# First norms on ScalarE, both parts of the forget weights side by side, and the cumulative sums placed later, in a two-block transformer kernel

## The chip, the cores and the metric

The kernel runs on one core of one Trainium2 chip. The metric is the device time of one execution in microseconds, taken as the median of several runs.

## The reference

Two transformer blocks work on 256 tokens of width 1024; in the first, 16 learned meta tokens stand ahead of them, so L = 272. Only the head of the first block matters here:

```python
h = jnp.concatenate([meta, x], axis=1)
hn = rms_norm(h, ln_pre_mix[layer])
proj = jnp.einsum('bld,dc->blc', hn, w_in[layer])
...
f_b = proj[..., OFF_VB:] + b_forget[layer].astype(proj.dtype)
o_a = swa_sink_attention(q_a, k_a, v_a, sinks[layer], rel_bias)
o_b = forgetting_attention(q_b, k_b, v_b, f_b)
```

`forgetting_attention` has 8 heads. It forms `cum = cumsum(log_sigmoid(f_logit))` along the sequence and adds `cum[t] - cum[s]` to the score of query t and key s. `swa_sink_attention` has 8 query heads and 2 key heads, a window of 128 tokens, and a bias per head that is read from a table of 32 buckets by distance. Behind both stand the output projection, a feed-forward part, and the second block.

## The kernel before, in words

All activations of the first block are kept transposed, as 8 slices of 128 channels by 272 tokens. Each number is held as a high part (`xh`, rounded to the format that TensorE takes at full speed) and a low part (`xl`, the rest). Weights are split in the same way when they have been loaded: `load` (L107) issues a transfer on SP's queue into one of three buffers `x`, ScalarE writes the high part `hi` (L114), and VectorE or GpSimd subtracts it for the low part `lo` (L115). A projection of one weight tile is then 8 x 3 products: high by high, high by low, low by high (L151 to L153).

`start` (L289) loads the meta rows and the tokens, forms the sum of squares of each row, and from it the factor of the norm. The factor goes onto the diagonal of a 128 x 128 matrix, and a product of the token rows with it scales and transposes at once (L327). Then the gain of the norm is applied (L621), the high part taken by ScalarE (L622) and the low part by VectorE or GpSimd (L623). Within the `with self.in_order(...)` block the order on VectorE, ScalarE and TensorE is the order of the code.

`first_block` (L684) follows. It projects the forget logits (weights `w_f`, 8 columns), then the tiles of `w_in` in the order of the plan at L692: tiles 6 to 9 are the queries of the forgetting attention, 10 to 13 its keys, 14 to 17 its values, 0 to 5 belong to the window attention. `uq(c)` projects tile 6 + c, `uk(c)` tile 10 + c. `cumulate1` transposes the log-sigmoids `fz` and `cumulate2` sums them by products with a triangular matrix; ScalarE copies the sums into `cum` and the negated ones into `ncum`, and two transfers on GpSimd's queue put them into row 64 of `qf` (queries) and row 65 of `kf` (keys). The scores of one pair of heads (L452) are products of 66 rows of `qf` and `kf`, so they add the sums by themselves, and they need both transfers.

`t5_bias` builds the bias of the window attention: a product with the bucket table, a copy by ScalarE into `t5qa` (L421), a transfer into DRAM (`t5vec`, L423), one that makes 32 copies of it there (`t5scr`, L426), and 16 that read these with shifted offsets into `bias` (L433). All of these are issued on GpSimd's queue (POOL), one behind the other.

The attention of four head pairs and then of four more runs as a pipeline of steps; `fills` names what is projected in each step. A step's fills stand ahead of the scores of its pair. Outside of the block that keeps the order of the code, a scheduler decides in which order each engine's instructions, and those of the queues, are written; on the chip each engine and each queue then takes them in that order.

Of the kernel before, what the change touches and what calls it, by code (L numbers as in the profile page):

```python
# [10 lines left out]
F32 = mybir.dt.float32  # L11
F32R = mybir.dt.float32r
# [4 lines left out]
AF = mybir.ActivationFunctionType  # L17
OP = mybir.AluOpType
AX = mybir.AxisListType
DRAM = bass.MemoryType.DRAM  # L20

D = 1024
# [24 lines left out]
NE1 = 'DDDD'  # L47
NE2='DADA'
NE3 = 'DDDD'
WM0 = 13  # L50
WM2 = 0
XO = 0
T5C = 32
# [11 lines left out]
FA = 1  # L65
FB = 0
FO = 0
CA, CB = 2, 3
KLT = 4
LATF = (12, 14, 16, 18)  # L70

C_PRE_MIX, C_PRE_FFN, C_BADA, C_C, C_QN, C_KVN, C_OA, C_OB = 0, 8, 16, 64, 72, 74, 75, 79
NCOLS = 83


class Body:
# [129 lines left out]
    def setup(self):  # L206
        nc, t, c = self.nc, self.t, self.const
        self.eps = c.tile([128, 1], F32, name="eps")
        nc.vector.memset(self.eps, EPS)

        nc.scalar.activation(self.sm([128, 1]), self.eps, AF.Sqrt)
        self.ident = c.tile([128, 128], F32, name="ident")
        self.cols = c.tile([128, NCOLS], F32, name="cols")

        self.xhb = c.tile([128, KT * L1 + NM], F32R, name="xh")
        self.xlb = c.tile([128, KT * L1 + NM], F32R, name="xl")
        self.xh, self.xl = (x[:, :KT * L1].rearrange("p (k n) -> p k n", k=KT) for x in (self.xhb, self.xlb))
        self.csil = c.tile([128, KT], F32, name="csil")
        self.modT = c.tile([128, 32], F32, name="modT")
        self.nx, self.nh, self.nl = 3, 4, 4  # L220
        self.rooms = False
        self.strm = self.ctx.enter_context(self.tc.tile_pool(name="strm", bufs=1, reuse_waits="tile"))

        self.hctx = ExitStack()
        hp = self.hctx.enter_context(self.tc.tile_pool(name="hp", bufs=1, reuse_waits="tile"))
        self.h = hp.tile([128, 2, D], F32, name="h")
        self.rn = hp.tile([128, T], F32, name="rn")
        self.ones = hp.tile([128, 128], F32, name="ones")
        nc.gpsimd.memset(self.ones, 1.0)
        self.hd = self.dram.tile([128, 2, D], F32, name="hd")  # L230
# [58 lines left out]
    def start(self, pool):  # L289

        nc, t = self.nc, self.t

        m = pool.tile([128, 4, T], F32, name="meta", tag="qa")[:NM].rearrange("p a b -> p (a b)")
        nc.sync.dma_start(m, t["meta"])
        half = [slice(hf * 512, (hf + 1) * 512) for hf in range(2)]
        for tt in range(2):
            for d in half:
                nc.sync.dma_start(self.h[:, tt, d], t["x"][tt * 128:(tt + 1) * 128, d])
        nc.sync.dma_start(self.ident, t["ident"])
        nc.sync.dma_start(self.cols, t["cols"])  # L300
        sm = self.sm([128, 1])[:NM]
        ym = pool.tile([128, KT, NM], F32, name="ymeta")
        y = pool.tile([128, 8, 288], F32, name="y", tag="bias").rearrange("p a b -> p (a b)")
        y = y[:, :2 * D].rearrange("p (t k n) -> p t k n", t=2, k=KT)
        gain = self.cols[:, C_PRE_MIX:C_PRE_MIX + KT, None]

        def norm(tt):

            ss, v, q, s = (self.sm([128, 1], tag=f"start{n}", bufs=2) for n in range(4))
            a, b = (self.h[:, tt, d] for d in half)  # L310
            self.square_sum(ss, a)
            nc.vector.tensor_scalar(v, ss, 1.0 / D, EPS, op0=OP.mult, op1=OP.add)
            sc = pool.tile([128, 2, 512], F32, name=self.nm("sqv"), tag="vf")[:, 0]
            nc.vector.tensor_tensor_reduce(sc, b, b, 1.0, 0.0, op0=OP.mult, op1=OP.add, accum_out=q)
            nc.scalar.activation(s, q, AF.Sqrt, scale=1.0 / D, bias=v)
            nc.vector.scalar_tensor_tensor(v, q, 1.0 / D, v, op0=OP.mult, op1=OP.add)
            return s, [lambda: nc.vector.reciprocal(s, s), lambda: nc.vector.tensor_mul(q, s, s),
                       lambda: nc.vector.scalar_tensor_tensor(q, q, -0.5, v, op0=OP.mult, op1=OP.mult),
                       lambda: nc.vector.scalar_tensor_tensor(s, q, 1.5, s, op0=OP.add, op1=OP.mult)]

        def scaled(x, n, r, banks, w):

            d = pool.tile([128, 128], F32, name=self.nm("diag"), tag="diag", bufs=3)[:n, :n]
            nc.vector.tensor_scalar(d, self.ident[:n, :n], r, None, op0=OP.mult)
            for k in range(KT):
                p, o = banks[k // w], k % w * n
                nc.tensor.matmul(p[:, o:o + n], lhsT=x[:, k * 128:(k + 1) * 128], rhs=d, start=True, stop=True)  # L327

        def gained(p, tt, hf, low, later=None):
            k, o = slice(hf * 4, hf * 4 + 4), tt * (128 + NM)  # L330
            self.gained(p[hf], y[:, tt, k], C_PRE_MIX + hf * 4, self.xh[:, k, o:o + 128], self.xl[:, k, o:o + 128], low, later)

        pw = self.bank()
        pm = self.bank()
        p0, p1 = ([self.bank() for _ in range(2)] for _ in range(2))
        mt = slice(128, 128 + NM)
        with self.in_order(mybir.EngineType.PE):
            self.warm(WM0, pw)
            self.square_sum(sm, m)
            rm = self.rstd(sm, 1, D)  # L340
            r0, steps = norm(0)
            for f in steps:
                f()
            scaled(self.h[:, 0], 128, r0, p0, 4)
            scaled(m, NM, rm, [pm], KT)
            r1, steps = norm(1)
            steps.pop(0)()
            gained(p0, 0, 0, nc.gpsimd)
            for f in steps:
                f()  # L350
            scaled(self.h[:, 1], 128, r1, p1, 4)
            gained(p0, 0, 1, nc.gpsimd)
            nc.vector.tensor_tensor(ym, pm[:, :KT * NM].rearrange("p (k n) -> p k n", k=KT),
                                    gain.to_broadcast([128, KT, NM]), op=OP.mult)
            nc.scalar.activation(self.xh[:, :, mt], ym, AF.Copy)
            nc.vector.tensor_sub(self.xl[:, :, mt], ym, self.xh[:, :, mt].bitcast(F32))
            self.fetch(1, nc.vector)
            if FO == 0:
                self.fetch(1, nc.gpsimd)
            self.warm(WM2, pw)  # L360
            late = []
            gained(p1, 1, 0, nc.vector, late)
            if FO == 1:
                self.fetch(1, nc.gpsimd)
            gained(p1, 1, 1, nc.vector, late)
            if FO == 2:
                self.fetch(1, nc.gpsimd)
            for f in late:
                f()
            self.fetch(1, nc.vector)  # L370

    def proj(self, out, wh, wl, apart):

# [252 lines left out]
    def scaled(self, xn, r, tt, hf):  # L626

        d = slice(hf * 512, (hf + 1) * 512)
        self.nc.vector.tensor_scalar(xn[:, d], self.h[:, tt, d], r, None, op0=OP.mult)
        return self.transposed4(xn, hf)  # L630
# [53 lines left out]
    def first_block(self):  # L684
        nc, t = self.nc, self.t
        w = self.work
        def win(*cs):
            return [("w_in", c, 1024) for c in cs]

        def wout(*cs):  # L690
            return [("w_out", c, 1024) for c in cs]
        self.plan(("w_f", None, 64), *win(6, 10, 7, 11, 8, 12, 9, 13, 14, 15, 4, 16, 5, 0, 17, 1, 2, 3),  # L692
                  *wout(4, 5, 6, 7, 0, 1, 2, 3))
        actx = ExitStack()
        self.attn = A = actx.enter_context(self.tc.tile_pool(name="attn1", bufs=1, reuse_waits="tile"))
# [4 lines left out]
        nc.gpsimd.memset(kf[64:66], 1.0)  # L700
        zz = A.tile([128, 5, 32], F32, name="zz")
        nc.gpsimd.memset(zz, 0.0)
        self.start(A)
        self.bias = A.tile([128, 8, 288], F32, name="bias", tag="bias")
        nc.sync.dma_start(bf, t["b_forget"])

        f = self.proj_tile("w_f", m=8, n=L1)
        z = A.tile([8, L1], F32, name="fz")
        nc.scalar.activation(z, f, AF.Identity, bias=bf)
        az = A.tile([8, L1], F32, name="faz")  # L710
# [66 lines left out]
                late.pop(0)()  # L777

        def uq(c):
            p = self.proj_tile("w_in", 6 + c, real=True)  # L780
            flush()
            for hd in range(2):
                nc.scalar.activation(qf[:64, 2 * c + hd], p[hd * 64:(hd + 1) * 64], AF.Copy, scale=0.125)

        def uk(c):
            p = self.proj_tile("w_in", 10 + c, n=L1)
            flush()
            for hd in range(2):
                nc.scalar.activation(kf[:64, 2 * c + hd], p[hd * 64:(hd + 1) * 64], AF.Copy)
# [48 lines left out]
        for i, (f, c) in enumerate(((uq, 0), (uk, 0), (uq, 1), (uk, 1))):  # L838
# [5 lines left out]
        vf = A.tile([128, 2, 512], F32, name="vf", tag="vf")  # L844
        do = lambda f, *a: (lambda: f(*a))
        fills = {
            0: [do(uq, 2), do(uk, 2)],
            1: [do(uq, 3), do(uk, 3), do(uv, 0)],
            2: [do(uv, 1), uka],
            3: [do(uv, 2), uva, do(uqa, 0)],  # L850
            4: [do(uv, 3), do(uqa, 1)],
# [25 lines left out]
        def gained(p, tt, hf, by, later=None):  # L877
            k, q = slice(hf * 4, hf * 4 + 4), slice(tt * 128, (tt + 1) * 128)
            self.gained(p[hf], y[:, tt, hf], C_PRE_FFN + hf * 4, self.xh[:, k, q], self.xl[:, k, q], by, later)
# [993 lines left out]
```

## Time and profile before

| | |
|---|---|
| median of 3 runs | 1260.43 us (1260.41 to 1262.22) |
| the profiled execution, its time | 1261.71 us |
| its span, first to last instruction | 1259.4 us |
| TensorE busy (PE) | 1230.8 us, 98% |
| VectorE busy (DVE) | 959.1 us, 76% |
| ScalarE busy (ACT) | 679.9 us, 54% |
| GpSimd busy (POOL) | 30.9 us, 2% |
| mean granted clock of TensorE | 0.997 |

Times in the profile count from the span's start. A busy TensorE may hide short waits, since the ends of products are modelled. In a row of the timeline the start stands first, then the duration of the group, the engine, the line, the operation, what it writes and reads, and how many instructions the group has; in square brackets the idle time ahead of it and what ended it. "SPq" and "POOL ... DMA" are issues of transfers.

### The profile page before, as it was taken

The numbers are of one execution on the slowest core, as the hardware profiler recorded it, in microseconds if no ns is written. First come the engines' busy times: TensorE is split into PE (matmuls) and PEld (weight loads), VectorE is DVE, ScalarE is ACT, GpSimd is POOL, SyncE is SP. The second block draws the span as 40 slices with busy tenths as digits, with TensorE's granted clock in tenths as the row PEclk, the third lists the DMA queues.
The fourth block names the chain that finished last, engine by engine and source line by source line (L and its number), as shares of the span: only waits on it lengthen the run. The fifth ranks groups of instructions, "written<-read, shape, count | busy, mean of one in ns | idle before, by whom it ended". The sixth has DMA issues, their size and how long they took to land.

```text
span 1259.4 us, 22080 instructions
## 1 busy us (share of the span) xinstructions
PE 1230.8 (98%) x8424; PEld 1102.8 (88%) x8424; DVE 959.1 (76%) x1923; ACT 679.9 (54%) x1268; POOL 30.9 (2%) x40
## 2 busy tenths in 40 slices
PE   8999999999999999999999999999999999999997
PEld 7887899999785499999999999999988888888885
DVE  5679887787878669998889999997555855555555
ACT  6655644454667355447566655545445545445453
POOL 2300200000000000000000000000000000000000
PEclk9999999999999999999999999999999999999999
DMA  6756588878261156565555544556676866656662
GB/s 223 212 203 220 178 289 281 272 264 296 83 191 62 34 191 198 176 188 174 171 165 166 152 153 151 158 151 196 197 253 212 306 199 189 197 184 189 196 195 90
DMA packets 67845, 239.44 MB, mean 190 GB/s; under 512 B 8499, under 2 KB 9155, under 8 KB 67452
## 3 DMA queue, kind: packets, MB, share of 16 engines
q1 hardware_dynamic: 66236, 233.00, 57.7%
q0 software_dynamic: 1216, 4.51, 1.2%
q8 instruction: 66, 1.08, 0.3%
q10 hardware_dynamic: 288, 0.52, 0.1%
q14 instruction: 39, 0.32, 0.1%
HBM read 235.87 MB, written 2.79 MB: 190 GB/s over the span
## 4 chain that ended last, share of the span: by engine, by line
PE 72%; DVE 15%; ACT 5%; DMA 5%; issue 3%; SPq 0%; POOL 0%; ACTq 0%; DVEq 0%
PE ps L151 19%; PE ps L153 19%; PE ps L152 19%; DVE lo L115 4%; ACT hi L114 3%; DVE W L1596 3%; PE ps L574 2%; DMA x<-in_w_gu 2%; PE ps L377 2%; PE ps L379 2%; PE ps L380 2%; PE ps L452 1%; DMA x<-in_w_down 1%; DVE al L1579 1%; PE ps L507 1%
## 5 line engine op out<-in xcount | busy, mean ns | idle before, releaser
L115 DVE TENSOR_TENSOR lo<-x,hi 128x1024 fp32r<-128x1024 f32 (+2 forms) x373 | 451.1, 1212 | 195.8 <-ACT hi L114 193.0
L114 ACT ACTIVATE hi<-x 128x1024 fp32r<-128x1024 f32 (+2 forms) x376 | 394.1, 1051 | 347.2 <-PE ps L153 171.0
L151 PE MATMUL ps<-xh,hi 128*128 128x256 f32 (+2 forms) x1296 | 373.6, 288 | 1.0 <-ACT xh L622 1.0
L152 PE MATMUL ps<-xl,hi 128*128 128x256 f32 (+2 forms) x1296 | 364.1, 281 | 1.5 <-DVE xl L623 1.5
L153 PE MATMUL ps<-xh,lo 128*128 128x256 f32 (+2 forms) x1296 | 364.4, 281 | 0.0
L152 PEld LDWEIGHTS ps<-xl,hi 128*128 128x128 f32 (+1 forms) x1296 | 244.0, 188 | 2.0 <-POOL lo L115 1.7
L151 PEld LDWEIGHTS ps<-xh,hi 128*128 128x128 f32 (+1 forms) x1296 | 243.2, 188 | 2.0 <-ACT xh L622 1.2
L153 PEld LDWEIGHTS ps<-xh,lo 128*128 128x128 f32 (+1 forms) x1296 | 243.3, 188 | 0.4 <-DVE lo L115 0.2
L151 PE MATMUL ps<-hi,w 128*128 128x512 f32 x512 | 199.6, 390 | 0.0
L153 PE MATMUL ps<-hi,w 128*128 128x512 f32 x512 | 199.2, 389 | 0.0
L152 PE MATMUL ps<-lo,w 128*128 128x512 f32 x512 | 199.2, 389 | 0.0
L152 PEld LDWEIGHTS ps<-lo,w 128*128 128x128 f32 x512 | 96.1, 188 | 20.2 <-issue 0.2
L151 PEld LDWEIGHTS ps<-hi,w 128*128 128x128 f32 x512 | 96.1, 188 | 20.1 <-ACT hi L114 0.2
L153 PEld LDWEIGHTS ps<-hi,w 128*128 128x128 f32 x512 | 96.1, 188 | 19.9
L377 PE MATMUL ps<-xh,hi 128*128 128x256 f32 x352 | 99.4, 283 | 0.6 <-ACT xh L622 0.6
L380 PE MATMUL ps<-xh,lo 128*128 128x256 f32 x352 | 98.6, 281 | 0.0
L379 PE MATMUL ps<-xl,hi 128*128 128x256 f32 x344 | 96.7, 281 | 0.0
L1598 ACT ACTIVATE W<-ps 128x352 f32<-128x352 f32 (+31 forms) x64 | 35.2, 554 | 68.8 <-DVE W L1596 68.7
L377 PEld LDWEIGHTS ps<-xh,hi 128*128 128x128 f32 x352 | 66.2, 188 | 1.6 <-ACT xh L622 0.9
L380 PEld LDWEIGHTS ps<-xh,lo 128*128 128x128 f32 x352 | 66.3, 188 | 0.0
L379 PEld LDWEIGHTS ps<-xl,hi 128*128 128x128 f32 x344 | 64.9, 189 | 0.7
L1596 DVE SCALAR_TENSOR_TENSOR W<-ps,W 128x160 f32<-128x160 f32 (+31 forms) x64 | 54.7, 861 | 11.8 <-ACT W L1635 11.5
(365 smaller groups left out, 1578.2 us busy)
## 6 DMA issues: line engine op xcount, KB each, us to landing
x<-in_u SPq DMA_DIRECT2D x128, 512.0 KB, 3.6
x<-in_v SPq DMA_DIRECT2D x128, 512.0 KB, 4.2
x<-in_w_gu SPq DMA_DIRECT2D x44, 512.0 KB, 4.5
ada<-in_w_ada SPq DMA_DIRECT2D x40, 512.0 KB, 5.0
x<-in_w_down SPq DMA_DIRECT2D x22, 512.0 KB, 4.4
x<-in_w_in SPq DMA_DIRECT2D x18, 512.0 KB, 4.3
x<-in_w_out SPq DMA_DIRECT2D x16, 512.0 KB, 4.4
x<-in_w_query SPq DMA_DIRECT2D x16, 512.0 KB, 3.6
```

Of the source, the lines that this page charges most:

```text
L114: nc.scalar.activation(hi[:, :w], x[:, :w], AF.Copy)
L115: low.tensor_sub(lo[:, :w], x[:, :w], hi[:, :w].bitcast(F32))
L151: mm(out, lhsT=lh, rhs=rh, start=start, stop=False)
L152: mm(out, lhsT=lh, rhs=rl, start=False, stop=False)
L153: mm(out, lhsT=ll, rhs=rh, start=False, stop=stop)
L377: mm(out, lhsT=wh[:, s], rhs=self.xh[:, k, :T], start=k == 0, stop=False)
L379: mm(out, lhsT=wh[:, s], rhs=self.xl[:, k, :T], start=False, stop=False)
L380: mm(out, lhsT=wl[:, s], rhs=self.xh[:, k, :T], start=False, stop=not apart and k == KT - 1)
L452: nc.tensor.matmul(S[tl, hd], lhsT=qT(tl, hd), rhs=kT(hd, n), start=True, stop=True)
L574: self.nc.tensor.matmul(acc[tt][hf], lhsT=o[:, tt * 128:(tt + 1) * 128], rhs=w[:, hf * 512:(hf + 1) * 512], start=start, stop=stop)
L1596: nc.vector.scalar_tensor_tensor(a, pv[:, :, :i0], 1.0 / GSC, a, op0=OP.mult, op1=OP.mult)
L1598: nc.scalar.activation(W[:, i0:, tk].rearrange("p i t -> p t i"), pv[:, :, i0:], AF.Copy, scale=1.0 / GSC)
```

## The change

- The meta rows are loaded on ScalarE's queue, the token rows come first on SP's, the identity matrix between the two row tiles. The forget weights get a buffer of their own (`wfx`), not one of the three for weight tiles.
- Squares of the tokens are summed by ScalarE alone, those of the meta rows by VectorE. The meta rows are scaled by ScalarE with their factor and then transposed, behind both token tiles, where before they went through a diagonal matrix between them. Warming products: 11 ahead and 4 behind, where 13 stood ahead.
- All low parts of this norm, and of the first weight tiles, are VectorE's; GpSimd computes nothing there.
- High and low part of the forget weights stand side by side as 16 columns. They are multiplied with `xh` and `xl` (16 products where 24 stood), and a product with `sel` adds the two halves.
- The projections of tiles 6 and 10 are written out in the ordered block, part by part: all products with high parts first.
- `cumulate1` runs behind `uk(1)` where it ran ahead of it; `cumulate2` is a fill of the first step behind `uq(2)`, where it ran ahead of `t5_bias`. `uq(3)` is moved from the second step into the first, so ahead of the first scores.

```diff
-WM0 = 13
+WM0 = 11
...
-CA, CB = 2, 3
+CA, CB = 3, 4
...
-        nc.sync.dma_start(m, t["meta"])
+        nc.scalar.dma_start(m, t["meta"])
+
+        nc.scalar.activation(self.sm([128, 1]), self.eps, AF.Sqrt)
...
-        nc.sync.dma_start(self.ident, t["ident"])
+            if tt == 0:
+                nc.sync.dma_start(self.ident, t["ident"])
         nc.sync.dma_start(self.cols, t["cols"])
+        self.wf = pool.tile([128, KT, 8], F32, name="wfx")
+        nc.sync.dma_start(self.wf, t["w_f"].rearrange("p (k n) -> p k n", k=KT))
...
+        def products(p, n, w, x, start=False, stop=False):
+
+            o = p[:, :n]
+            if n == T:
+                o = o.rearrange("p (a b) -> p a b", a=2)
+            for k in range(KT):
+                b = x[:, k * L1:k * L1 + n] if n == L1 else x[:, k * L1:k * L1 + 288].rearrange("p (a b) -> p a b", a=2)[:, :, :128]
+                mm(o, lhsT=w[:, k * 128:(k + 1) * 128], rhs=b, start=start and k == 0, stop=stop and k == KT - 1)
+
+        wf = pool.tile([128, KT, 2, 8], F32R, name="wf")
+
+        def forget(x, start=False, stop=False):
+
+            for k in range(KT):
+                mm(pf[:16, :L1], lhsT=wf[:, k].rearrange("p s n -> p (s n)"), rhs=x[:, k], start=start and k == 0, stop=stop and k == KT - 1)
...
+            scaled(self.h[:, 1], r, p1)
+            nc.scalar.activation(m, m, AF.Copy, scale=rm)
+            for k in range(KT):
+                nc.tensor.transpose(pm[:, k * NM:(k + 1) * NM], m[:, k * 128:(k + 1) * 128], self.ident[:NM, :NM])
+            nc.scalar.activation(wf[:, :, 0], self.wf, AF.Copy)
+            nc.vector.tensor_sub(wf[:, :, 1], self.wf, wf[:, :, 0].bitcast(F32))
+            self.warm(4, pw)
+            late = []
+            for tt, p in enumerate((p0, p1)):
+                for hf in range(2):
+                    gained(p, tt, hf, nc.vector, late)
...
+            self.fetch(3, nc.vector)
+            uq, uk = self.unit("w_in", 6, False), self.unit("w_in", 10, False)
+            forget(self.xh, start=True)
+            products(pq, T, uq[0], self.xhb, start=True)
+            forget(self.xl, stop=True)
+            nc.scalar.activation(fs, pf[:16, :L1], AF.Copy)
+            products(pq, T, uq[1], self.xhb)
+            products(pq, T, uq[0], self.xlb, stop=True)
+            f = self.bank()[:8, :L1]
+            mm(f, lhsT=sel, rhs=fs, start=True, stop=True)
+            products(pk, L1, uk[0], self.xhb, start=True)
+            products(pk, L1, uk[1], self.xhb)
+            products(pk, L1, uk[0], self.xlb, stop=True)
+        self.made = {6: pq[:, :T], 10: pk[:, :L1]}
+        return f
...
-        self.plan(("w_f", None, 64), *win(6, 10, 7, 11, 8, 12, 9, 13, 14, 15, 4, 16, 5, 0, 17, 1, 2, 3),
+        self.plan(*win(6, 10, 7, 11, 8, 12, 9, 13, 14, 15, 4, 16, 5, 0, 17, 1, 2, 3),
...
-            0: [do(uq, 2), do(uk, 2)],
-            1: [do(uq, 3), do(uk, 3), do(uv, 0)],
+            0: [do(uq, 2), cumulate2, do(uk, 2), do(uq, 3)],
+            1: [do(uk, 3), do(uv, 0)],
```

Three places show how the instructions move. The first is GpSimd's queue from the first transfer on, before (the numbers behind names are buffer numbers):

```order
L744 DMA qf<-cum 1x16x128
L746 DMA kf<-ncum 1x8x272
L423 DMA t5vec<-t5qa 8x656
L426 DMA t5scr<-t5vec 32x5248
L433 DMA bias<-t5scr 32x8x128 x2
L433 DMA bias<-t5scr 32x8x16 x2
```

The last two rows stand there four times in turn, 16 transfers in all. The same queue after the change, where they stand four times as well:

```order
L465 DMA t5vec<-t5qa 8x656
L468 DMA t5scr<-t5vec 32x5248
L785 DMA qf<-cum 1x16x128
L475 DMA bias<-t5scr 32x8x128 x2
L475 DMA bias<-t5scr 32x8x16 x2
L787 DMA kf<-ncum 1x8x272
```

The transfer of the sums into `qf` has moved behind two transfers of the bias chain, that of the negated sums into `kf` behind all 18.

The second place is ScalarE from the high part of tile 9's weights on, before and after:

```order
L114 ACTIVATE hi_476<-x_475 128x1024
L114 ACTIVATE hi_509<-x_508 128x1024
L789 ACTIVATE kf<-ps_404 64x272
L742 ACTIVATE cum<-ps_431 8x272
L743 ACTIVATE ncum<-ps_431 8x272
L421 ACTIVATE t5qa<-ps_447 8x384
L421 ACTIVATE t5qa<-ps_450 8x272
```

```order
L127 ACTIVATE hi_460<-x_459 128x1024
L830 ACTIVATE kf<-ps_392 64x272
L463 ACTIVATE t5qa<-ps_431 8x384
L463 ACTIVATE t5qa<-ps_434 8x272
L127 ACTIVATE hi_503<-x_502 128x1024
L127 ACTIVATE hi_536<-x_535 128x1024
L824 ACTIVATE qf<-ps_465 64x256
L783 ACTIVATE cum<-ps_492 8x272
L784 ACTIVATE ncum<-ps_492 8x272
```

The copies of the bias table have moved ahead of the sums, and two further weight tiles (13 and 14) and the queries of tile 8 stand between them.

The third place is TensorE from the program's start on, before and after:

```order
L147 MATMUL ps_116<-ones 128x128 x13
L327 MATMUL ps_118<-diag_163,h 128x128 x4
L327 MATMUL ps_119<-diag_163,h 128x128 x4
L327 MATMUL ps_117<-diag_173,meta 128x16 x8
L327 MATMUL ps_120<-diag_201,h 128x128 x4
L327 MATMUL ps_121<-diag_201,h 128x128 x4
L151 MATMUL ps_244<-xh,hi_218 8x272
```

```order
L160 MATMUL ps_118<-ones 128x128 x11
L328 MATMUL ps_120<-diag_162,h 128x128 x4
L328 MATMUL ps_121<-diag_162,h 128x128 x4
L328 MATMUL ps_122<-diag_191,h 128x128 x4
L328 MATMUL ps_123<-diag_191,h 128x128 x4
L384 MATMUL ps_119<-ident,meta 128x16 x8
L160 MATMUL ps_118<-ones 128x128 x4
L358 MATMUL ps_124<-xh,wf 16x272 x8
L351 MATMUL ps_125<-xh,hi_232 128x256 x8
```

The meta products have moved behind the second token tile, and the first projections stand part by part.

## Rows read from the trace of the kernel before

**Rows 1.** Waits of TensorE up to 120 us: engine, line, releaser: us, times, longest

```profile
PE ps L152 <- DVE xl L623: 1.5, 1, 1.5
PE ps L327 <- DVE diag L324: 1.4, 1, 1.4
...
PE ps L452 <- DMA kf<-ncum: 0.8, 1, 0.8
```

**Rows 2.** Busy time by stretch: stretch, length, PE, PEld, DVE, ACT, POOL, clock, DMA

```profile
50.00:75.00 25.00, 25.00 (x194) 23.25 (x192) 17.74 (x58) 13.62 (x32) 5.51 (x10) 1.00 0.73 219
75.00:100.00 25.00, 24.64 (x196) 19.87 (x196) 22.08 (x81) 14.34 (x41) 0.00 (x0) 1.00 0.57 186
```

**Rows 3.** Timeline of the first 40 us, TensorE's rows

```profile
1.00 5.11 PE L147 MATMUL ps<-ones 128*128 128x128 f32 x26 [1.00 <-POOL ones L229]
...
7.47 2.05 PE L327 MATMUL ps<-diag,h 128*128 128x128 f32 x16 [1.36 <-DVE diag L324]
...
9.46 1.95 PE L327 MATMUL ps<-diag,meta 16*128 16x16 f32 x16
...
16.30 0.29 PE L152 MATMUL ps<-xl,hi 128*8 128x272 f32 x1 [1.50 <-DVE xl L623]
```

**Rows 4.** Line 623 up to 200 us: ns min/median/max, first and last start

```profile
L623 DVE TENSOR_TENSOR xl<-y,xh x4: 678/1174/1784, 14.4 to 138.0; 128x512 fp32r<-128x512 f32 x4
```

**Rows 5.** Timeline of TensorE from 24.5 and from 31 us

```profile
25.00 0.28 PE L152 MATMUL ps<-xl,hi 128*128 128x256 f32 x1
...
27.37 0.28 PE L151 MATMUL ps<-xh,hi 128*128 128x256 f32 x1
...
31.25 1.63 PE L739 MATMUL ps<-tri,lst 128*8 128x272 f32 x6
32.82 1.27 PE L420 MATMUL ps<-t5vf,rel 33*8 33x384 f32 x4
```

**Rows 6.** Timeline of ScalarE, 22 to 60 us

```profile
30.64 1.06 ACT L114 ACTIVATE hi<-x 128x1024 fp32r<-128x1024 f32 x1 [1.15 <-DMA x<-in_w_in]
...
35.76 0.74 ACT L421 ACTIVATE t5qa<-ps 8x384 f32<-8x384 f32 x2
```

**Rows 7.** Timeline of GpSimd's queue, 0 to 60 us

```profile
35.89 0.74 POOL L744 DMA_DIRECT2D qf<-cum  x1 [20.27 <-ACT ncum L743]
36.62 0.55 POOL L746 DMA_DIRECT2D kf<-ncum  x1
37.15 0.52 POOL L423 DMA_DIRECT2D t5vec<-t5qa  x1
41.26 0.52 POOL L426 DMA_DIRECT2D t5scr<-t5vec  x1 [3.59 <-DMA t5vec<-t5qa]
46.23 7.55 POOL L433 DMA_DIRECT2D bias<-t5scr  x13 [4.45 <-DVE pm L482]
54.18 1.73 POOL L433 DMA_DIRECT2D bias<-t5scr  x3 [0.40 <-DMA bias<-t5scr]
```

**Rows 8.** Chain that ended last, 20 to 62 us: start, us, what

```profile
36.62 4.18 DMA kf<-ncum
...
40.94 1.65 PE ps L452 x8
...
45.42 0.13 PE ps L151
```

**Rows 9.** Busy time by stretch, around a lower clock (columns as in rows 2)

```profile
384.00:386.00 2.00, 2.00 (x10) 1.61 (x10) 0.81 (x2) 2.00 (x10) 0.00 (x0) 0.50 0.00 0
```

**Rows 10.** Timeline of TensorE, 378 to 392 us

```profile
379.24 1.14 PE L452 MATMUL ps<-kT,qT 64*128 64x256 f32 x8
...
383.34 0.44 PE L507 MATMUL ps<-ident,sb 128*128 128x128 f32 x2 [1.95 <-DVE sb L489]
...
385.51 2.04 PE L452 MATMUL ps<-kT,qT 64*128 64x256 f32 x8
```

**Rows 11.** The transfers that write bias: landing times

```profile
DMA to landing us min/median/max: 2.4/5.2/6.4
```

More of the change, by code (lines that the diff above doesn't have):

```diff
@@ L73, with __init__, tensor_sub, run @@
 NCOLS = 83
+class Later:
+    def __init__(self, engine):
+        self.engine, self.todo = engine, []
+    def tensor_sub(self, *a):
+        self.todo.append(lambda: self.engine.tensor_sub(*a))
+    def run(self):
+        while self.todo:
+            self.todo.pop(0)()
 class Body:
@@ L209, in setup @@
         nc.vector.memset(self.eps, EPS)
-        nc.scalar.activation(self.sm([128, 1]), self.eps, AF.Sqrt)
         self.ident = c.tile([128, 128], F32, name="ident")
@@ L305, in start, with scaled @@
         gain = self.cols[:, C_PRE_MIX:C_PRE_MIX + KT, None]
[L307 to L324, printed above, removed]
+        def scaled(x, r, banks):
+            d = pool.tile([128, 128], F32, name=self.nm("diag"), tag="diag", bufs=2)
+            nc.vector.tensor_scalar(d, self.ident, r, None, op0=OP.mult)
             for k in range(KT):
-                p, o = banks[k // w], k % w * n
-                nc.tensor.matmul(p[:, o:o + n], lhsT=x[:, k * 128:(k + 1) * 128], rhs=d, start=True, stop=True)
+                nc.tensor.matmul(banks[k // 4][:, k % 4 * 128:(k % 4 + 1) * 128], lhsT=x[:, k * 128:(k + 1) * 128], rhs=d, start=True, stop=True)
         def gained(p, tt, hf, low, later=None):
@@ L336, in start @@
         mt = slice(128, 128 + NM)
+        pf, pq, pk = (self.bank() for _ in range(3))
+        sel = pool.tile([16, 8], F32, name="sel")
+        fs = pool.tile([16, L1], F32, name="fs")
+        ss = [self.sm([128, 2], tag=f"start{n}", bufs=1) for n in range(2)]
+        mm = nc.tensor.matmul
+        def products(p, n, w, x, start=False, stop=False):
[5 more added lines that the diff above has]
+                mm(o, lhsT=w[:, k * 128:(k + 1) * 128], rhs=b, start=start and k == 0, stop=stop and k == KT - 1)
@@ L337, in start @@
+        wf = pool.tile([128, KT, 2, 8], F32R, name="wf")
+        def forget(x, start=False, stop=False):
+            for k in range(KT):
+                mm(pf[:16, :L1], lhsT=wf[:, k].rearrange("p s n -> p (s n)"), rhs=x[:, k], start=start and k == 0, stop=stop and k == KT - 1)
         with self.in_order(mybir.EngineType.PE):
             self.warm(WM0, pw)
-            self.square_sum(sm, m)
-            rm = self.rstd(sm, 1, D)
-            r0, steps = norm(0)
+            sc = pool.tile([128, 2, 512], F32, name="sqm", tag="vf")[:NM].rearrange("p a b -> p (a b)")
+            nc.vector.tensor_tensor_reduce(sc, m, m, 1.0, 0.0, op0=OP.mult, op1=OP.add, accum_out=sm)
+            self.h_squares(ss[0], 0, 0)
+            r, steps = self.rstd2(ss[0])
+            steps.pop(0)()
+            self.h_squares(ss[0], 0, 1)
+            steps.pop(0)()
@@ L342, in start @@
             for f in steps:
                 f()
[L344 to L348, printed above, removed]
+            rm, steps = self.rstd_steps(sm, 1, D)
+            scaled(self.h[:, 0], r, p0)
+            nc.vector.tensor_reduce(sel, self.ident[:16, :16].rearrange("p (g c) -> p c g", g=2), axis=AX.X, op=OP.add)
             for f in steps:
                 f()
-            scaled(self.h[:, 1], 128, r1, p1, 4)
@@ L352, in start @@
-            gained(p0, 0, 1, nc.gpsimd)
+            self.h_squares(ss[1], 1, 0)
+            r, steps = self.rstd2(ss[1])
+            steps.pop(0)()
+            self.h_squares(ss[1], 1, 1)
+            for f in steps:
+                f()
+            scaled(self.h[:, 1], r, p1)
[3 more added lines that the diff above has]
+            nc.scalar.activation(wf[:, :, 0], self.wf, AF.Copy)
@@ L355, in start @@
             nc.scalar.activation(self.xh[:, :, mt], ym, AF.Copy)
[L356 to L367, printed above, removed]
             for f in late:
                 f()
-            self.fetch(1, nc.vector)
+            nc.vector.tensor_sub(self.xl[:, :, mt], ym, self.xh[:, :, mt].bitcast(F32))
+            self.fetch(3, nc.vector)
[13 more added lines that the diff above has]
+        return f
     def proj(self, out, wh, wl, apart):
@@ L702, in first_block @@
         nc.gpsimd.memset(zz, 0.0)
-        self.start(A)
+        f = self.start(A)
         self.bias = A.tile([128, 8, 288], F32, name="bias", tag="bias")
         nc.sync.dma_start(bf, t["b_forget"])
-        f = self.proj_tile("w_f", m=8, n=L1)
         z = A.tile([8, L1], F32, name="fz")
@@ L779, in uq @@
         def uq(c):
-            p = self.proj_tile("w_in", 6 + c, real=True)
+            p = self.proj_tile("w_in", 6 + c, real=True) if 6 + c not in self.made else self.made[6 + c]
             flush()
@@ L785, in uk @@
         def uk(c):
-            p = self.proj_tile("w_in", 10 + c, n=L1)
+            p = self.proj_tile("w_in", 10 + c, n=L1) if 10 + c not in self.made else self.made[10 + c]
             flush()
```

## The prediction

> **What bounds the kernel now.** I read the waits of TensorE first. Up to 120 us it is stopped by name only for short times, among them 1.5 us for a low part in the first norm, 1.4 us for the first diagonal and 0.8 us for the transfer that puts the negated cumulative sums into kf [rows 1]. The table by stretch comes next: from 50 to 75 us TensorE is busy without a gap, and from 75 to 100 us it idles 0.36 us [rows 2]. So in this first block a microsecond lost or won on TensorE before 50 us arrives at the end. The timeline of the start shows where its dense products begin, at 16.30 us, and what lies ahead of them [rows 3]. The GpSimd timeline shows the queue on which the change puts things into another order [rows 7], and the chain of waits shows where that queue meets TensorE: the kf transfer is issued at 36.62 us, takes 4.18 us, and the first scores of the forgetting attention start behind it at 40.94 us [rows 8]. The next tile's query products (tile 9, the last one for queries) follow the scores and end at 45.42 us, where the key products of tile 13 begin [rows 8]. This last point is my **marker**: before the change, both the first scores and tile 9 are done at 45.42 us. After it their order is the other way round, and what follows on TensorE is the same in both kernels. So the shift of the marker is the change of the whole, unless later idle time takes some of it up.
>
> **The start.** The token rows are issued one place earlier on the SP queue, since meta goes out on ScalarE's queue. I put the first scaled transposes half a microsecond earlier, at 7.0 instead of 7.47 us. They take 2.05 us per row tile [rows 3]. The meta products stood between the two tiles for 1.95 us [rows 3]; they move behind them. I let the second tile start at 9.6 us, when its diagonal can be ready, so it is done at 11.65. The meta transposes are bounded by half of the old price, 0.98 us (they need one pass where a product of full numbers needs two: each of the eight shows as two of the 16 there), and the whole of it, 1.95 us. Four more warming products follow, each 5.11/13 = 0.39 us [rows 3], so 1.6 us. Dense products can begin at 14.1 us, at the latest at 15.2. GpSimd no longer subtracts there: on VectorE that subtraction took between 678 and 1784 ns [rows 4], and I take the lower end, since GpSimd then runs nothing beside it. Four of them, four gains, and three full low parts on VectorE fall in time with TensorE's first products, which are ordered so that high parts come first. I cost this at nothing; if the cover fails, 1.5 us as in [rows 1].
>
> **TensorE from there to the scores.** Twenty products of 256 columns took 27.37 - 25.00 = 2.37 us [rows 5], 0.1185 each, and I take 0.126 for 272 columns. The forget weights cost 16 x 0.126 = 2.0 us where 24 x 0.126 = 3.0 stood; the selecting product costs about a third of 1.63 us [rows 5], 0.54. Up to the end of the bias-table products: 14.1 + 2.0 + tile 6 (24 x 0.1185 = 2.84) + 0.54 + tile 10 (3.02) + tile 7 (2.84) + tile 11 (3.02) + small transposes (0.36 at most) + the table products (1.27 [rows 5]) = 30.0 us. Behind them stand tile 8 (2.84), the cumulative sums (1.63), tile 12 (3.02) and tile 9 (2.84), so TensorE itself is ready for the first scores at 40.3 us.
>
> **The GpSimd queue, where the time goes.** The changed queue has the bias chain first: table to DRAM (t5vec), its 32 copies (t5scr), 16 transfers into bias, and only behind all of them the kf transfer. The first scores wait for that one, and TensorE works in order, so everything stands behind them. ScalarE copies the table after it has split tile 9's weights. That split waited 1.15 us for a load in its old place, and the table's copies take 0.74 us [rows 6]; so t5vec goes out between 30.7 and 31.9 us, and I take 31.3. From here I use the old distances [rows 7]: 41.26 - 37.15 = 4.11 us to t5scr, 46.23 - 41.26 = 4.97 us to the first bias transfer, 55.91 - 46.23 = 9.68 us for the 16 of them (13 in 7.55 us, a wait of 0.40, 3 in 1.73). The kf transfer is then issued at 50.1, lands after 4.18, and scores start 0.14 us later [rows 8], at 54.4 us. TensorE has then stood still for 14 us. The scores take 1.65 us [rows 8], so the marker is passed at 56.0 us: **10.6 us later than before**.
>
> **The clock.** Before the change the granted clock is at 0.50, that is 1.2 of 2.4 GHz, between 384 and 386 us [rows 9], just after TensorE had waited 1.95 us for VectorE; the same group of attention scores then took 2.04 instead of 1.14 us [rows 10]. A wait of 14 us should leave it there. The cost is bounded by nothing and by 3.4 us (two such stretches, each losing half of some 3.4 us). I take one of them, 1.7 us, the middle.
>
> **The sum.** 10.6 + 1.7 = 12.3 us. The profiled execution, whose rows these are, took 1261.71 us with a span of 1259.4; the median of the three runs is 1260.43, so 1.28 lower. I put the shift on the median: **1272.7 us**.
>
> Bounds. Low: t5vec at 30.7, the 16 transfers without their wait, no clock loss: 10.6 - 0.6 - 0.4 = 9.6, 1270.0. High: dense products at 15.2 (+1.1), a second late load (+1.2), the kf transfer landing like the slowest bias transfer, 6.4 us [rows 11], so +2.2, two stretches of slow clock (+1.7): 12.3 + 6.2 = 18.5, 1278.9.
>
> Now the short transfers of that queue. In rows, t5vec keeps the queue waiting until 4.11 us after its issue, and kf, a few KB, lands after 4.18 us [rows 7, 8]. The Trainium skill, page "DMA: Bandwidth & Descriptors", section on the anatomy of one DMA on the GpSimd path, fits a transfer by a fixed 2.0 us and its bytes over 436 GB/s. By that both would take about half, and 1272.7 would become some 1268.5 as an estimate. The traces here do not agree, with about 4 us for each; I keep the rows.
>
> **The rivals.**
> 1. *No wait forms, and the kernel is faster.* If the kf transfer lands by the time TensorE has done its own work (40.3 us), the marker is passed at 40.3 + 1.65 = 42.0, 3.4 us earlier: 1257.0. For it: the start is shorter and the sums have two more tiles of products as cover. Against it: it decides at an issue of kf before 36 us, and the 16 bias transfers that precede it on its own queue take 9.68 us after a chain of 9.1 us [rows 7]. Chance 0.04.
> 2. *The transfers land sooner.* The fastest bias transfer landed after 2.4 us [rows 11]. With t5vec and kf at 2.4 instead of 4.1, 3.4 us go: 1269.3. The page named above would say this. Against it: two of two short ones took 4. Chance 0.08.
> 3. *The loss is partly taken up later.* Between 75 and 100 us weight loading idles 5 of 25 us [rows 2], so some stretch there may be set by others than TensorE. That could take up at most these 5.1 us: 1267.6. Against it: VectorE and ScalarE stand behind the same scores and shift along. Chance 0.06.
> 4. *The wait is longer.* Each of the last bias transfers, and kf, also waits until the one eight places ahead has landed; the 0.40 us in rows 7 are such a wait. With landings of 6.4 us, several of these and two slow stretches of clock: 1278.9. Chance 0.10.
> 5. *The start's gain and the wait cancel.* This needs a wait of about 4 us in place of 14, for which I see no row. Chance 0.02.
>
> **How the numbers follow.** The forecast has 0.70 for itself (1270 to 1276). A measurement here can tell about 0.2%, 2.5 us, from no change. Only rival 1 gives faster (0.04) and rival 5 no change (0.02); all the rest, 0.94, is slower. The range runs from 1267.6, which takes in rivals 2 and 3, to 1277.5, which leaves out most of rival 4 and rivals 1 and 5.
>
> **What would show it.** In the profile after: a wait of TensorE of 11 to 16 us before the first scores, put down to the kf transfer; on GpSimd that transfer's issue behind the 16th bias transfer at about 50 us; the granted clock at half in part of the 15 us after; dense products beginning near 14 us; from the first scores on the old timeline, 11 to 13 us later. If the wait before the first scores is under 3 us, the prediction is wrong at its main step; if the shift is there at 60 us and gone at 130, rival 3 holds.

## The result and the profile after

The changed kernel takes **1274.41 us** (median of four runs, 1271.92 to 1277.8) where the kernel before, run beside it, takes 1261.14 (four runs, 1260.41 to 1262.22). The ratio is **1.0099, 95% interval 1.0084 to 1.0114**: slower by 12.5 us by the ratio and by 13.3 us between the two medians. The profiled run took 1275.04 us, with a span of 1273.0 (before 1259.4) and a mean granted clock of 0.99.

The waits of TensorE over the whole span come first: engine, line, releaser, then us in total, times, and the longest.

```profile
PE ps L494 <- DMA kf<-ncum: 13.6, 1, 13.6
...
PE ps L164 <- ACT zh L1009: 1.7, 1, 1.7
```

Line 494 is the line of the forgetting scores, 452 before. What was a stop of 0.8 us [rows 1] is one of 13.6 us, and its releaser is the same transfer. The wait of 1.5 us for a low part in the first norm [rows 1] is gone.

Where those 13.6 us were made is seen on GpSimd's queue. Its timeline from 25 to 60 us gives start, duration, line, operation, count, and in brackets the idle time ahead and what ended it.

```profile
30.22 0.65 POOL L465 DMA_DIRECT2D t5vec<-t5qa  x1 [25.23 <-ACT t5qa L463]
35.63 0.55 POOL L468 DMA_DIRECT2D t5scr<-t5vec  x1 [4.76 <-DMA t5vec<-t5qa]
36.22 0.57 POOL L785 DMA_DIRECT2D qf<-cum  x1
41.91 4.63 POOL L475 DMA_DIRECT2D bias<-t5scr  x8 [5.12 <-DMA t5scr<-t5vec]
46.95 4.60 POOL L475 DMA_DIRECT2D bias<-t5scr  x8 [0.41 <-DMA bias<-t5scr]
51.54 0.54 POOL L787 DMA_DIRECT2D kf<-ncum  x1
```

Before, the two rows of qf and kf stood first and the table's chain behind them [rows 7]. Now kf is last. The qf transfer, which the same scores need, got past on the way (36.22), so only one of the two sums is late. The chain that ended last goes down this queue and meets TensorE at its end (start, us, what):

```profile
41.91 4.76 DMA bias<-t5scr
...
51.54 1.75 DMA kf<-ncum
53.29 0.14 issue
53.42 3.11 PE ps L494 x8
...
63.65 1.41 PE ps L494 x8
```

The scores took 3.11 us where they took 1.65 [rows 8]. The table by stretch says why (stretch, length, busy PE, PEld, DVE, ACT, POOL, then granted clock, DMA share, GB/s):

```profile
45.00:50.00 5.00, 0.00 (x0) 0.00 (x0) 0.00 (x0) 0.00 (x0) 4.59 (x9) 0.50 0.75 151
53.40:58.80 5.40, 5.38 (x19) 4.93 (x20) 1.52 (x9) 1.31 (x6) 0.00 (x0) 0.50 0.00 0
58.80:62.00 3.20, 3.20 (x28) 3.20 (x27) 1.74 (x7) 1.97 (x6) 0.00 (x0) 0.98 0.00 0
75.00:100.00 25.00, 25.00 (x199) 22.34 (x199) 18.91 (x64) 13.24 (x32) 0.00 (x0) 1.00 0.53 175
```

From 45 to 50 us no compute engine does anything but issue transfers on GpSimd. TensorE then works at 0.50, that is 1.2 GHz, until 58.8 us, and at full clock after. From 75 to 100 us it is busy throughout, where the kernel before idled 0.36 us in that window [rows 2]; the loss is not taken up there.

The start did get shorter. TensorE's timeline:

```profile
6.91 2.05 PE L328 MATMUL ps<-diag,h 128*128 128x128 f32 x16 [1.64 <-DVE diag L326]
9.21 2.05 PE L328 MATMUL ps<-diag,h 128*128 128x128 f32 x16 [0.24 <-DVE diag L326]
11.19 0.66 PE L384 MATMUL ps<-ident,meta 16*128 16x16 f32 x8
11.79 1.16 PE L160 MATMUL ps<-ones 128*128 128x128 f32 x8
12.91 1.16 PE L358 MATMUL ps<-xh,wf 128*16 128x272 f32 x8
...
14.91 1.14 PE L358 MATMUL ps<-xl,wf 128*16 128x272 f32 x8
```

Dense products begin at 12.91 us and have no gap behind them, where they began at 16.30 [rows 3].

**The account by places.** I take the second group of forgetting scores as a fixed place. After the change it stands at 63.65 us in the chain above, before at 51.44, so 12.2 us are lost:

```profile
51.44 1.41 PE ps L452 x8
```

The first scores begin at 53.42 instead of standing with tile 9 done at 45.42 - 1.65 = 43.77 us, so the late transfer is 9.65 of them. The other 2.56 are the clock: 1.46 in the scores (3.11 - 1.65) and 1.10 in the products behind them (7.12 us from the marker, at 56.53, to the second group, 6.02 before). The span is 13.6 longer; 1.2 of the remaining 1.4 us stand as a longer wait in the feed-forward part, for `zh`, before and then after:

```profile
320.39 0.50 PE L151 MATMUL ps<-hi,zh 128*128 128x512 f32 x1 [0.48 <-ACT zh L968]
333.68 0.50 PE L164 MATMUL ps<-hi,zh 128*128 128x512 f32 x1 [1.73 <-ACT zh L1009]
```

That this comes from the late transfer is not shown. Experiments 2 and 3 below, with waits for kf of 14.5 and 17.9 us, have no such wait of TensorE for `zh`, and experiment 5, with one of 2.0 us, has 2.3 us of it.

### The profile page after: what moved, and what is told of

The parts are those of the page before. It is cut to its first block, busy times and chain, and to the rows that moved or that the text cites. A ratio compares the mean times of both kernels' runs of the same rounds, so it can differ in the third digit from the quotient of the medians.

```text
span 1273.0 us, 22065 instructions
## 1 busy us (share of the span) xinstructions
PE 1232.8 (97%) x8414; PEld 1104.8 (87%) x8414; DVE 960.3 (75%) x1924; ACT 681.2 (54%) x1272; POOL 25.9 (2%) x37
## 4 chain that ended last, share of the span: by engine, by line
PE 77%; DVE 11%; DMA 5%; ACT 4%; issue 2%; POOL 0%; ACTq 0%; DVEq 0%; SPq 0%; POOLq 0%
PE ps L164 21%; PE ps L166 21%; PE ps L165 20%; DVE lo L128 3%; DMA x<-in_w_gu 2%; PE ps L616 2%; ACT hi L127 2%; PE ps L419 2%; PE ps L422 2%; PE ps L421 2%; DVE W L1637 1%; PE ps L494 1%; DMA x<-in_w_down 1%; PE ps L549 1%; PE ps L1627 1%
## 5 line engine op out<-in xcount | busy, mean ns | idle before, releaser
L128 DVE TENSOR_TENSOR lo<-x,hi 128x1024 fp32r<-128x1024 f32 (+1 forms) x373 | 452.0, 1215 | 198.2 <-ACT hi L127 195.7
L127 ACT ACTIVATE hi<-x 128x1024 fp32r<-128x1024 f32 (+1 forms) x375 | 393.6, 1053 | 351.4 <-PE ps L166 167.3
L164 PE MATMUL ps<-xh,hi 128*128 128x256 f32 (+1 forms) x1272 | 368.5, 290 | 0.0
L166 PE MATMUL ps<-xh,lo 128*128 128x256 f32 (+1 forms) x1272 | 358.6, 282 | 0.0
L165 PE MATMUL ps<-xl,hi 128*128 128x256 f32 (+1 forms) x1272 | 357.3, 281 | 0.0
L164 PEld LDWEIGHTS ps<-xh,hi 128*128 128x128 f32 x1272 | 240.2, 189 | 1.1 <-issue 0.9
L165 PEld LDWEIGHTS ps<-xl,hi 128*128 128x128 f32 x1272 | 240.8, 189 | 0.1
L166 PEld LDWEIGHTS ps<-xh,lo 128*128 128x128 f32 x1272 | 239.8, 189 | 0.0
L419 PEld LDWEIGHTS ps<-xh,hi 128*128 128x128 f32 x352 | 66.2, 188 | 1.6 <-ACT xh L664 0.9
L422 PEld LDWEIGHTS ps<-xh,lo 128*128 128x128 f32 x352 | 66.3, 188 | 0.0
L421 PEld LDWEIGHTS ps<-xl,hi 128*128 128x128 f32 x344 | 64.9, 189 | 0.7
```

The costliest lines, as they stand in the source:

```text
L127: nc.scalar.activation(hi[:, :w], x[:, :w], AF.Copy)
L128: low.tensor_sub(lo[:, :w], x[:, :w], hi[:, :w].bitcast(F32))
L164: mm(out, lhsT=lh, rhs=rh, start=start, stop=False)
L165: mm(out, lhsT=lh, rhs=rl, start=False, stop=False)
L166: mm(out, lhsT=ll, rhs=rh, start=False, stop=stop)
L419: mm(out, lhsT=wh[:, s], rhs=self.xh[:, k, :T], start=k == 0, stop=False)
```

## The experiments

My theory: one transfer's place on GpSimd's queue (kf behind the table's chain) costs the time, plus the clock behind the wait; the new start and the later sums are not to blame. Rivals: that the later sums themselves are late, whatever the queue; that the start loses something; that the clock term is none.

**1. The start alone** (label start_only). The change without the later sums:

```diff
-CA, CB = 3, 4
+CA, CB = 2, 3
...
-            0: [do(uq, 2), cumulate2, do(uk, 2), do(uq, 3)],
-            1: [do(uk, 3), do(uv, 0)],
+            0: [do(uq, 2), do(uk, 2)],
+            1: [do(uq, 3), do(uk, 3), do(uv, 0)],
```

> The changed kernel with the sums back in their old places (CA, CB = 2, 3, the old fills), so the new start alone. Theory: the start is a gain of some 3 us: first scores near 38 us, 1257.5 to 1259 us. Rival (the new start costs, for instance by low parts that come too late on VectorE): 1261 us or more.

Measured: 1257.08 us, ratio to the kernel before **0.9967 [0.9954, 0.9981]**. Repeated beside experiment 8 it gave 1257.72 and 0.9965 [0.9951, 0.9978]. This is faster than both kernels. GpSimd's timeline and the chain:

```profile
32.70 0.55 POOL L787 DMA_DIRECT2D kf<-ncum  x1
33.22 0.52 POOL L465 DMA_DIRECT2D t5vec<-t5qa  x1
```

```profile
36.96 1.41 PE ps L494 x8
47.23 1.41 PE ps L494 x8
```

With kf ahead of the chain there is no wait for it at all. The second group stands at 47.23 us, 4.2 us earlier than before, which is the gain by the ratio (0.33%); the medians differ by 4.9. So the start gains and does not lose. Which of its parts gives how much of it I didn't take apart.

**2. The later sums alone** (label sums_only): before.py's kernel with the two lines of the order of work from the change, CA, CB = 3, 4 and the new fills.

> The kernel before with only the sums moved (CA, CB = 3, 4, the new fills), so the old start. Theory: the kf transfer again stands behind the 16 bias transfers, issued near 55 us, first scores near 57 us, 1276 to 1279 us, more than the whole change since the start gains nothing. Rival (moving the sums alone costs little, the two parts only cost together): 1261 to 1266 us.

Measured: 1279.6 us, **1.0142 [1.0127, 1.0157]**, 0.6 us above what I expected. The wait and the transfer's issue:

```profile
PE ps L452 <- DMA kf<-ncum: 14.5, 1, 14.5
```

```profile
57.28 0.54 POOL L746 DMA_DIRECT2D kf<-ncum  x1
```

The loss of about 17.9 us is that of the change plus the gain of the start (12.5 + 4.2 = 16.7) within the intervals. What loses is the move.

**3. Only the transfer moved** (label kf_last). The kernel before, with its sums, products and start where they were; only kf's transfer is put behind the table's chain on the same queue. The 16 transfers into bias are kept in the order of the code, so that kf stays behind them (cut here):

```diff
-            nc.gpsimd.dma_start(kf[65:66], ncum)
+            sums.append(lambda: self.tc.keep_in_program_order(nc.gpsimd.dma_start(kf[65:66], ncum)))
...
         self.t5_bias(A)
+        sums.pop()()
```

> The kernel before with one transfer moved and nothing else: kf is issued behind the 16 bias transfers. Theory (that one place in the queue is the loss): kf is issued near 56 us, lands after 1.8 us as in the changed kernel, first scores near 58 instead of 41 us, and with the lower clock behind it 1280 to 1284 us. Rival (the loss needs the other moves as well): 1262 to 1270 us.

Measured: 1280.89 us, **1.0144 [1.0125, 1.0162]**: as much as the whole move. The waits, then the queue:

```profile
PE ps L452 <- DMA kf<-ncum: 17.9, 1, 17.9
```

```profile
48.38 9.24 POOL L433 DMA_DIRECT2D bias<-t5scr  x16 [6.02 <-DMA t5scr<-t5vec]
57.61 0.53 POOL L748 DMA_DIRECT2D kf<-ncum  x1
```

One transfer in another place on its queue gives the loss. The rest is as good as unchanged: TensorE's and VectorE's instructions stand in the order of the kernel before up to 100 us, and on ScalarE the split of a weight tile stands a few places later.

**4. The transfer put ahead of the 16** (label kf_first). The change, with the 16 transfers into bias issued behind the cumulative sums:

```diff
-        self.t5_bias(A)
+        spread = self.t5_bias(A)
...
-            0: [do(uq, 2), cumulate2, do(uk, 2), do(uq, 3)],
+            0: [do(uq, 2), cumulate2, spread, do(uk, 2), do(uq, 3)],
```

Inside t5_bias the loops that issue the 16 transfers become the function spread.

> The changed kernel with one thing altered: the 16 bias transfers are emitted behind the sums, so that the kf transfer stands ahead of them on GpSimd's queue, behind t5vec and t5scr. Theory (the whole loss is TensorE waiting for kf behind the bias chain): kf is issued near 36.8 us, lands near 41, the first scores wait 1 to 2 us instead of 13.6, the clock stays at 1.00 there, and the time is 1257.5 to 1259.5 us, faster than before. Rival (the earlier bias chain collides with the loads of weights, or the new start itself costs): 1265 us or more.

Measured: 1262.49 us, 1.0001 [0.9988, 1.0014], between the theory and the rival. The loss is gone, but none of the gain of the start is there; I had expected most of it, and the clock at 1.00. The chain and the stretch behind:

```profile
35.99 6.73 DMA kf<-ncum
42.85 3.08 PE ps L497 x8
53.71 1.41 PE ps L497 x8
```

```profile
45.00:50.00 5.00, 5.00 (x23) 4.77 (x22) 2.62 (x14) 1.92 (x8) 3.66 (x8) 0.53 0.62 129
```

The transfer was issued at 35.99 us, early enough, but took 6.73 us: ahead of it on its queue, with only qf's few KB between them, stands t5scr, which writes 656 KB. TensorE waited 3.0 us, and behind this wait too the clock was low, 0.53 from 45 to 50 us. The second group stands at 53.71 us, 6.5 us later than in experiment 1: the wait and the slower work behind it use up the whole gain.

**5. The transfers on ScalarE's queue** (label kf_act): the change with nc.scalar.dma_start for qf's and kf's rows in place of nc.gpsimd.dma_start.

> The changed kernel with the two transfers of the sums (into qf and kf) on ScalarE's queue, the bias chain alone on GpSimd's. Theory (only the queue matters: behind the bias chain kf was issued late, and behind t5scr on the same queue it landed late, 6.73 us): kf is issued near 36.5 us, lands by 40 us, TensorE waits under 1 us, the clock stays at 1.00, 1257 to 1259 us, as good as the start alone. Rival (moving the sums under the roots costs by itself, through the bias chain beside the loads): 1260 us or more.

Measured: 1260.02 us, 0.998 [0.9967, 0.9992], one microsecond over what I expected and at the rival's lower bound, so this run does not decide between the two; experiment 8 does. The profiled run was the slowest of its twelve (1266.72), so its wait of 2.0 us need not be the usual one:

```profile
36.72 5.00 DMA kf<-ncum
41.86 3.11 PE ps L494 x8
```

Another queue takes the long wait away too. The transfer still took 5.00 us while t5scr, issued at 35.69 us on GpSimd's queue, was on its way; that the one slows the other is likely but not shown. Again a short wait is followed by scores at half clock.

**6. The clock behind the long wait** (labels warm, warm66). The change, with products whose result nobody reads, kept on TensorE between its last own work and the scores, 46 of them and then 66:

```diff
+        def keep_busy():
+            p = self.bank()
+            for _ in range(66):
+                self.tc.keep_in_program_order(nc.tensor.matmul(p[:, :128], lhsT=self.ones, rhs=self.ident, start=True, stop=True, skip_group_check=True))
...
-            0: [do(uq, 2), cumulate2, do(uk, 2), do(uq, 3)],
+            0: [do(uq, 2), cumulate2, do(uk, 2), do(uq, 3), keep_busy],
```

> The changed kernel with 46 products of the ones by the identity matrix, whose result nothing reads, ahead of the first scores, so that TensorE works while it waits for kf. Theory (the wait costs twice, by itself and by the lower clock behind it): the granted clock stays at 1.00 and the first scores take 1.65 instead of 3.11 us, 1271 to 1272.5 us. Rival (the clock costs nothing in the end): 1274 to 1275 us; if the products run past the landing of kf, up to 1277.

With 46: 1275.8 us, 1.0100 [1.0078, 1.0121]. In the profiled run they ended after some 10 us, 5.2 us of waiting were left, and the clock fell in those; the scores took 3.11 us. Two of the six executions took 1270.6 and 1271.2 us at a mean granted clock of 0.996, the other four 1275.8 to 1278.5 at 0.993 to 0.994. A trace is kept of one of the four alone, so whether the wait differed is not known. This run told nothing certain of the clock's price, so I made the products longer.

> The changed kernel with 66 products that nothing reads ahead of the first scores; the 46 of the last try lasted 10 us and left 5.2 us of idle time behind them, in which the clock fell all the same. At 0.215 us each they last 14.2 us, until about 54 us. Theory (the lower clock costs 2.7 us behind the wait): clock 1.00 throughout, the first scores take 1.6 instead of 3.1 us, 1271 to 1273 us. Rival (it costs nothing in the end): 1274 to 1276 us.

With 66: 1271.44 us, 1.0076 [1.0060, 1.0092]. TensorE's timeline:

```profile
39.84 14.90 PE L891 MATMUL ps<-ident,ones 128*128 128x128 f32 x132
55.07 1.65 PE L494 MATMUL ps<-kf,qf 66*128 66x144 f32 x8 [0.34 <-DMA kf<-ncum]
```

and the second group in the chain:

```profile
62.73 1.41 PE ps L494 x8
```

The clock stayed at 1.00 and the scores took 1.65 us. The second group of scores follows 7.66 us behind the first (62.73 - 55.07) where it followed after 10.23 in the change: **2.6 us** is the clock's part, by the trace. The second group itself stands only 0.9 us earlier than in the change, because kf was issued 1.6 us later in this execution (53.17 us). The medians differ by 3.0 us, but the two intervals overlap, and the times do not separate the clock from the later issue: the 2.6 us rest on the traces.

**7. The same for the short wait** (label kf_first_warm): experiment 4 with 14 such products.

> The kernel with kf ahead of the bias transfers, which waited 3.0 us for kf and then ran 6.8 us at the lower clock, with 14 products (3.0 us) in that wait. Theory: the clock stays at 1.00, 3.4 us are won, 1258.5 to 1260 us. Rival (the lower clock is hidden by other waits): 1262 us, as without them.

Measured: 1260.87 us, 0.9993 [0.9981, 1.0005], between the theory and the rival. The chain:

```profile
36.50 6.98 DMA kf<-ncum
43.61 1.65 PE ps L497 x8
51.27 1.41 PE ps L497 x8
```

By the trace the second group is 2.4 us earlier than in experiment 4 (51.27 against 53.71) although the first starts 0.8 later. By the times the two kernels can't be told apart, since their intervals overlap; that the clock costs about 3 us behind a wait of 3 us rests on one execution of each.

**8. The later sums with the whole chain behind them** (label chain_last). If the theory holds, the move itself is harmless: the change, with t5vec, t5scr and the 16 transfers all issued behind the sums.

```diff
-            0: [do(uq, 2), cumulate2, do(uk, 2), do(uq, 3)],
+            0: [do(uq, 2), cumulate2, chain, do(uk, 2), do(uq, 3)],
```

Here chain calls what t5_bias issued, kf's and t5vec's transfers are kept in the order of the code, and `qa` is allocated behind the chain.

> The changed kernel with the whole bias chain (t5vec, t5scr, the 16 transfers) issued behind the two transfers of the sums. In the tries with kf behind t5scr, or on ScalarE's queue beside it, kf landed 5.0 to 7.0 us after its issue; in the kernel before it took 4.2 with nothing large ahead. Theory (what is left of the loss there is the 656 KB of t5scr ahead of kf): kf is issued near 36 us, lands near 40, a wait of TensorE under 1 us, clock 1.00, 1256.5 to 1259 us, like the start alone. Rival (moving the sums costs by itself, whatever the queue's order): 1260 us or more.

Measured: 1257.57 us, **0.9959 [0.9946, 0.9973]**, beside 0.9965 for the start alone on the same chip. GpSimd's timeline and the chain:

```profile
36.08 0.55 POOL L788 DMA_DIRECT2D kf<-ncum  x1
36.60 0.52 POOL L470 DMA_DIRECT2D t5vec<-t5qa  x1
39.50 0.52 POOL L471 DMA_DIRECT2D t5scr<-t5vec  x1 [2.37 <-DMA t5vec<-t5qa]
```

```profile
39.84 1.41 PE ps L495 x8
47.25 1.41 PE ps L495 x8
```

kf's transfer, from issue to landing:

```profile
DMA to landing us min/median/max: 2.9/2.9/2.9
```

With t5scr behind it and not ahead, kf landed after 2.9 us where it took 6.73 in experiment 4. TensorE doesn't wait for kf, and bias, which now begins at 45.03 us, is in time too. The second group stands at 47.25 us, as in the start alone (47.23). TensorE's instructions have the order that they have in the change, so only the queue differs there. So the sums in their new place cost nothing and gain nothing that can be measured: the rival that they are late by themselves falls.

**9. GpSimd back in the first norm** (label start_gps): experiment 1, with the first row tile's gains on GpSimd again.

```diff
-                    gained(p, tt, hf, nc.vector, late)
+                    gained(p, tt, hf, nc.vector if tt else nc.gpsimd, late)
```

> The new start alone, with the low parts of the first token tile back on GpSimd (the second tile's on VectorE). Theory (VectorE and GpSimd slow each other: 1.2 us instead of 0.62 for a low part on VectorE beside GpSimd): the products with low parts of the activations start 1 to 2 us later, 1258 to 1259.5 us. Rival (these low parts are hidden under the products with high parts): 1257 us.

Measured: 1258.76 us, 0.9971 [0.9958, 0.9984], not to be told from experiment 1. The low parts of this norm on VectorE, ns min/median/max, first and last start, in the change and then here:

```profile
L665 DVE TENSOR_TENSOR xl<-y,xh x4: 682/684/685, 12.1 to 13.9; 128x512 fp32r<-128x512 f32 x4
```

```profile
L665 DVE TENSOR_TENSOR xl<-y,xh x2: 680/1248/1815, 12.1 to 13.8; 128x512 fp32r<-128x512 f32 x2
```

Of the two subtractions that are left on VectorE, the one beside GpSimd's took 2.7 times as long. TensorE nevertheless came to its first product with a low part at 14.87 us, 14.91 in the change: the new order of products covers it, and the step of the theory that had them late is wrong, though the time lies in its range. What this trace has later is a wait of 1.2 us for the log-sigmoids, behind which the second group of scores stands at 48.41 us, not 47.23:

```profile
25.86 0.28 PE L773 MATMUL ps<-ident,fz 8*128 8x8 f32 x3 [1.22 <-DVE fz L763]
```

ScalarE took them up late, behind a weight tile whose load it had waited 0.98 us for. Whether GpSimd has a part in that isn't shown.

## Why the prediction was right

The time was forecast as 1272.7 us and measured as 1274.41, inside the range, by the mechanism that was named: kf behind the whole chain, TensorE standing still for it, and a lower clock behind the wait. That the number came so close is in part luck, since several terms were off and cancelled. The shift was forecast as 12.3 us and measured as 13.3 between the medians. Point by point, with what was foreseen first:

- **The start**: dense products at 14.1, measured 12.91. The meta transposes took 0.66 us, less than the lower bound of 0.98. That the low parts would be covered held (experiment 9). TensorE itself was ready for the scores at 53.42 - 13.6 = 39.8 instead of 40.3: of the 1.2 us won at the start, 0.7 went again, since the products up to there took 26.9 us and not 26.2.
- **The queue's order**: kf behind the 16th transfer, its issue at 50.1, measured 51.54. Two distances were longer than those taken over from [rows 7]: t5vec to t5scr 5.41 instead of 4.11, t5scr to the first bias transfer 6.28 instead of 4.97. The second was not the time of t5scr even before: the row names VectorE (`pm`) as what ended that wait, and t5scr had landed 4.3 us after its issue; in the change it took 5.67. The 16 themselves took 9.63 for 9.68, and the chain began 1.1 us earlier (30.22 for 31.3).
- **The landing of kf**: 4.18 taken from [rows 8], measured 1.75. This more than cancels the misses above: scores at 53.42, foreseen at 54.4. The Trainium skill, page "DMA: Bandwidth & Descriptors", section on the anatomy of one DMA on the GpSimd path, gives some 2 us for it; 1.75 agrees, but 4.18 before and 6.73 behind t5scr do not, and it names no term for what stands ahead in the queue. Rival 2, which took the two landings for short, was right for kf and wrong for t5vec (5.12 us).
- **The clock**: 1.7, one stretch like that in [rows 9]; measured 2.6, with the clock at 0.50 over the 5.4 us from 53.4 to 58.8. This term was undersized. The pure shift of the marker was 9.65 where 10.6 was foreseen, so the sum of the two came out right to 0.1 us: 12.2 for 12.3. Two errors cancelled there.
- **Later idle time**: rival 3 had the loss partly taken up; instead 1.4 us came on top by the spans, most of it a wait for `zh` whose cause stays open.
- **Rival 1** (no wait, 1257.0) is what experiments 1 and 8 made: 1257.08 and 1257.57. Its condition, kf issued before 36 us, was met in experiment 1 (32.70), where the sums are back in their old place, and missed by a hair in experiment 8 (36.08), where the order of the queue alone differs from the change. Experiment 4 shows that an issue time is the wrong condition: issued at 35.99, kf was late, since it landed after 6.73 us behind t5scr and after 2.9 us ahead of it.

## What to carry to other kernels

A small transfer that an engine in order waits for belongs ahead of every long chain on its queue: look, in the order of issue and not in the source, at what stands between its data being ready and its issue, and at how many bytes stand right ahead of it. Here its place ahead of the chain or behind it decided between 0.4% faster and 1% slower, with the same work on all compute engines (experiment 8 and the change). When costing a wait of TensorE, add the lower clock behind it, 2.6 us here.

## What the runs showed that I had not expected

- The same few KB of kf landed after 1.75 us behind bias transfers that had mostly landed, 2.9 in experiment 8, 4.18 before, 5.00 from ScalarE's queue, and 6.73 and 6.98 behind t5scr on GpSimd's. The 1.75 us fall in a stretch in which the core moved 57 GB/s in all (51.5 to 53.3 us), where it moved 163 in that of the kernel before, so what the queue does to a landing and what the other traffic does isn't separated.
- Waits of TensorE of 3.0 and 2.0 us (experiments 4 and 5) were followed by the lower clock, where I had expected 1.00, although [rows 9] and [rows 10] show it behind 1.95 us. It does not follow each such wait: in experiment 1 the same 1.95 us for `sb` end at 379.25 us, and the clock is at 1.00 from 378 to 384.
- Putting idle TensorE to work on products that nobody reads brought the second scores 0.9 us forward, though the first started 1.65 us later.
